# A decoder step on one core: decode key steps spread over two stages, their products over two engines, and norm operands moved to PSUM

## The chip, the cores and the metric

The kernel runs on one core of a Trainium2 chip. The core has a matrix engine (TensorE, PE in the profile, with its weight loads as PEld), a vector engine (VectorE, DVE), a scalar engine (ScalarE, ACT), a general engine (GpSimd, POOL) and a queue engine (SyncE, SP) that here issues all DMAs. Each engine takes its own instructions in the order in which the program gives them. The metric is the device time of one execution in microseconds.

## The reference

One inference step of a two-layer decoder, run for a prompt (1024 positions) and for 8 samples with one new position each, in float32, width 1024.

Layer 0 projects the input into queries, keys, values, gates and a pooling branch. Eight heads of 64 do stick-breaking attention:

```
z = q k^T / sqrt(64) + bias
log_keep = log_sigmoid(-z)            (only keys before the query)
w = exp(log_sigmoid(z) + sum of log_keep over the keys between this key and the query)
o = w v
```

The prompt attends to itself. Each sample attends to a cache of 4096 past keys and values, held in pages of 128 positions that a page table picks. The other branch is a multi-scale causal mean. Both are gated, projected by `w_out` and added to the input: `layer_norm(1.41 * x + o, g, b)`.

Layer 1 projects into three parts, gates one with another, runs a causal depthwise convolution with 31 taps, normalizes over the 1024 channels, applies SiLU, gates, projects by `w_out` and ends with the same kind of layer norm. The outputs are both groups' rows, the new keys and values, and the new pooling and convolution states.

## The kernel before, in words

Every float32 product of the projections is done as three products of split operands (high x high, high x low, low x high), so each weight piece is copied to a high part by ACT (line 205) and its rest is taken by POOL (line 210), and each activation is split likewise (lines 195 and 196). The prompt's rows stand in eight sets of 128 tokens.

The order on TensorE, ACT, DVE and POOL is the order in which the program emits instructions (`manual_schedule`); SP's queue is ordered by the framework's planner. The program runs in these stages:

1. A prologue, and then *attention* over 48 units (a head pair, a block of 128 queries, up to 512 keys). `z_a` makes the scores on TensorE and the sigmoids on ACT, `z_b` runs a scan and products on DVE (lines 365 to 371), `tpart` transposes the weights (line 845), `ppart` multiplies by the values (line 861). Between these, `fill.part` emits pieces of layer 0's input projection (lines 225 to 227).
2. The *out projection* of layer 0, `out_layer`: 32 groups of 24 matmuls (lines 1029 to 1031), each 128 tokens by 256 columns. After each group DVE adds the residual (line 1062) and takes statistics (1066). Two accumulators in PSUM, `acc()`, alternate; the first groups also use others. Once all four columns of a token set are done, its norm is put off for one or two groups and then emitted (`app`): a first op on DVE, (y - mean) x scale, `norm_a`; then either ACT and POOL, or on the fast path DVE again, for the factor of the deviation and the shift, `norm_b`. In layer 0 the scale stands in PSUM (`gps0`), so `norm_a` is two ops of 512 columns (line 1009); in layer 1 it stands in SBUF (line 1013).
3. Layer 1's input projection (`c_gen`) with the *convolution*: taps on DVE into a PSUM tile of two banks (`conv_acc`, tag "conv", line 1373) and on ACT and POOL; beside it `decode_v`, the samples' value products.
4. The *middle*: the convolution's norm. `mid_a` (lines 1555 and 1556) writes mean and deviation rows into one PSUM bank for each entry of `MID`, `mid_b` (line 1567) applies them on DVE, `mid_s` is SiLU on ACT, `mid_g` the gate on POOL or DVE (line 1588), `mid_c` the split (lines 195 and 196). PSUM banks shared for short use come from `trp()`, a ring of NZT banks in a pool that `swap_psum` replaces at each stage.
5. The *final projection* of layer 1, again `out_layer`, with the samples' path beside it, and the last norms.

Beside stages 1 and 2 runs `decode_k`, a generator of 155 steps that `tick(n)` advances. Two halves of 4 samples each have 64 units; a unit is two pages of keys. Step s loads unit s (line 405, four buffers `kt`), multiplies unit s - 2 by its query (line 417, on POOL or on DVE) and reduces unit s - 3 (line 409, DVE). After the 67 steps of a half come ten steps that finish it: transposes, sigmoids, a scan, a carry, and transposes back. The prologue gives 8 steps, each attention unit `TBASE + TSLOPE * (384 - keys) / 384`, each group of the out projection one, and the first 8 pieces of the next projection two each. What is then left runs alone.

Of the kernel before, what the change touches and what calls it, by code (L numbers as in the profile page):

```python
# [14 lines left out]
F32 = mybir.dt.float32  # L15
# [3 lines left out]
AF = mybir.ActivationFunctionType  # L19
ALU = mybir.AluOpType  # L20
AX = mybir.AxisListType
SP = mybir.EngineType.SP
PSUM = bass.MemoryType.PSUM

P = 128
D = 1024
S = 1024
# [18 lines left out]
KS = 30  # L46
PS_ = 15
NEG = -1e30
KMOD = 8
KPOOL = 7  # L50
ENG = mybir.EngineType
KLAG = 2
DTB = 2
# [12 lines left out]
WRB = 3  # L66
ETICK = 0.35
EDVE = (1, 2, 3, 0)
TBASE = 2.8
TSLOPE = 1.5  # L70
NHEADS = (0, 6, 6, 6, 6, 6, 6, 6)
SNY = 7
# [12 lines left out]
SNZ = 5  # L85
HALVES = (3, 6)
OLAG = 3
FAST = (5, 6, 7)
WCONVA = ((0, 5), (1, 5))
SY = 2  # L90
VRATE = 1.575
# [9 lines left out]
def kernel(  # L101
# [9 lines left out]
    pe, act, dve, gp, sp = nc.tensor, nc.scalar, nc.vector, nc.gpsimd, nc.sync  # L111
# [8 lines left out]
    w_out1 = w_out_c[0]  # L120
# [11 lines left out]
    pz = [pap.enter_context(tc.tile_pool(name="pza", bufs=1, space=PSUM))]  # L132
    NZT = [5]

    def psum(tag, bufs, shape=(P, 512), dt=F32):
        return (psq[0] if tag == "qv" else ps).tile(list(shape), dt, tag=tag, name=tag, bufs=bufs)
# [3 lines left out]
    def acc():  # L140
        deep[1] += 1
        if deep[0] and deep[1] % deep[0] == 0:
            return trp()
        return psum("acc", 2)

    def trp():
        return pz[0].tile([P, 512], F32, tag="zt", name="zt", bufs=NZT[0])

    def swap_psum(name, n):
        pzp.close()  # L150
        pz[0] = pzp.enter_context(tc.tile_pool(name=name, bufs=1, space=PSUM, reuse_waits="tile"))
        NZT[0] = n
# [63 lines left out]
    def dma_quarter(w, q, i):  # L216
        return dma_w(w[i * 256:(i + 1) * 256, q * 256:(q + 1) * 256], 2, 256)
# [171 lines left out]
    def decode_k():  # L389
        qrow = {0: query_rows(0)}  # L390
        yield
        for hf in range(2):
# [5 lines left out]
            for s in range(len(units) + KLAG + 1):  # L398
# [13 lines left out]
                if KLAG <= s < len(units) + KLAG:  # L412
                    bi, j = units[s - KLAG]
                    b = hf * 4 + bi
                    kt = kts[s - KLAG]
                    eng = gp if (j // 2) % KMOD < KPOOL else dve
                    eng.tensor_tensor(out=kt, in0=kt, in1=qrow[b], op=ALU.mult)  # L417
# [53 lines left out]
    def tick(n):  # L471
        while n > 0 and queue:
            try:
                next(queue[0])
                n -= 1
            except StopIteration:
                queue.pop(0)
# [328 lines left out]
    def z_a(u):  # L806
        pair, qb, c0, c1, first, last = units[u]
        n = c1 - c0
        nz = max(n, 256)
        km = KT[pair]  # L810
        sq, ql = SQ[pair, qb // 2]
        qs = slice(qb % 2 * P, qb % 2 * P + P)
        zs = [trp(), trp()]
        for hh in range(2):
            pe.matmul(zs[hh][:, 0:nz], sq[:, hh, qs], km[:, hh, c0:c0 + nz], start=True, stop=False)
        for hh in range(2):
            r = slice(hh * DH, hh * DH + DH)
            pe.matmul(zs[hh][:, 0:nz], ql[r, qs], km[r, hh, c0:c0 + nz], start=False, stop=not first)
        sk = []
        for hh in range(2):  # L820
            h = pair * 2 + hh
            if first:
                pe.matmul(zs[hh][:, n - P:n], identb, maskb, start=False, stop=True)
            kp = KP[u % 2 * 2 + hh]
            stick_a(zs[hh], kp, n, biash[:, h:h + 1], nbiash[:, h:h + 1])
            sk.append((zs[hh], kp))
        st["z", u] = sk
        if u in PREP:
            prep(*PREP[u])
# [62 lines left out]
    t = trp()  # L892
# [23 lines left out]
    for i, q in enumerate(qorder):  # L916
# [3 lines left out]
        o = acc()[:, 0:n]  # L920
# [26 lines left out]
    for u in range(len(units) + 2):  # L947
        if u < len(units):
# [6 lines left out]
            fcred += fbase  # L955
            tcred += TBASE + TSLOPE * (384 - n) / 384.0
            z_a(u)
# [47 lines left out]
    def norm_a(gb, y, mv, halves, gps):  # L1005
        if gps:
            for i in range(2):
                h = slice(i * 512, i * 512 + 512)
                dve.scalar_tensor_tensor(out=y[:, h], in0=y[:, h], scalar=mv[:, 0:1], in1=gps[i],
                                         op0=ALU.subtract, op1=ALU.mult)  # L1010
            return
        for h in halves:
            dve.scalar_tensor_tensor(out=y[:, h], in0=y[:, h], scalar=mv[:, 0:1], in1=gb[:, 0, h],
                                     op0=ALU.subtract, op1=ALU.mult)

    def norm_b(gb, y, rs, fast, h):
        if fast:
            dve.scalar_tensor_tensor(out=y[:, h], in0=y[:, h], scalar=rs, in1=gb[:, 1, h], op0=ALU.mult, op1=ALU.add)
        else:
            act.activation(out=y[:, h], in_=y[:, h], func=AF.Copy, scale=rs)  # L1020
            gp.tensor_tensor(out=y[:, h], in0=y[:, h], in1=gb[:, 1, h], op=ALU.add)  # L1021
# [10 lines left out]

    def out_layer(w, first, ahead, X, gb, pool, finish, between, before=None, half=None, tail=None, lag=OLAG, fast0=FAST, wide=0, gps=()):
        order = [(n4, tb) for t0 in (0, 4) for n4 in range(2) for tb in range(t0, t0 + 4)]
        for i in range(NTB + lag):
            if i < NTB:
                order.append((2, i))
            if i >= lag:
                order.append((3, i - lag))
        dmas = {0: (1, 3)} | {9 + i: (2, i) for i in range(4)} | {13 + i: (3, i) for i in range(4)}  # L1040
        convs = {i: (1, i) for i in range(4)} | {12 + i: (2, i) for i in range(4)} | {16 + i: (3, i) for i in range(4)}
        raws, sts = {}, {}
        tiles = {0: first, 1: [], 2: [], 3: []}

        def fetch(q, i):
            raws[q, i] = dma_quarter(w, q, i)

        for i in range(3):
            raws[1, i] = ahead[i]
        for s, (n4, tb) in enumerate(order):  # L1050
            f0 = n4 * 256
            if s in convs:
                q, i = convs[s]
                tiles[q].append(conv_w(raws[q, i], 2, 256, pool if q % 2 else None, dve if q == 1 and i % 2 and fast0 is FASTB else None))
            if s in dmas:
                fetch(*dmas[s])
            if before is not None:
                before(n4, tb)
            o = (trp() if s < wide and s % 3 else acc())[:, 0:256]
            out_group(tiles[n4], o, tb, half)  # L1060
            y = X[tb]
            dve.scalar_tensor_tensor(out=y[:, f0:f0 + 256], in0=y[:, f0:f0 + 256], scalar=ALPHA,
                                     in1=o, op0=ALU.mult, op1=ALU.add)
            if n4 == 0:
                sts[tb] = pool.tile([P, 4, 6], F32, tag="st", name="st", bufs=NTB)
            dve.bn_stats(sts[tb][:, n4, :], y[:, f0:f0 + 256])
            if n4 == 3:
                fast = tb in fast0
                halves = (slice(0, 512), slice(512, 1024)) if tb >= 6 else (slice(0, 1024),)
                mv, rs = norm_s(pool, sts[tb])  # L1070

                def app(y=y, mv=mv, rs=rs, tb=tb, fast=fast, halves=halves):
                    norm_a(gb[0], y, mv, halves, gps)
                    for h in halves:
                        norm_b(gb[0], y, rs, fast, h)
                        finish(tb, y, h)
                defer((DTC if fast0 is FASTB else DTD)[tb], app)
            between(n4, tb)
            point()
            if tail is not None:  # L1080
                tail(n4, tb)
# [4 lines left out]
    X = {}  # L1086
# [80 lines left out]
    rows = [(w_out0, 0, k) for k in range(NK)]  # L1167
# [347 lines left out]
    BC = {}  # L1515
# [34 lines left out]

    def mid_a(c):
        a, b = MID[c]
        t = trp()
        for i, tb in enumerate(range(a, b)):
            pe.transpose(out=t[:, i * P:(i + 1) * P], in_=rmf[:, tb:tb + 1].broadcast_to([P, P]), identity=ident)
            pe.transpose(out=t[:, 256 + i * P:256 + (i + 1) * P], in_=rvf[:, tb:tb + 1].broadcast_to([P, P]),
                         identity=ident)
        BC[c] = t
# [31 lines left out]
    X = {}  # L1590
# [5 lines left out]
            X[tb] = C[:, tb].rearrange("p k c -> p (k c)")  # L1596
            sp.dma_start(X[tb], x1_dram[tb * P:(tb + 1) * P, :])

    gb1 = [None]

    def before(n4, tb):
        if (n4, tb) in STEPS:
            STEPS[n4, tb]()
        if n4:
            return
        if tb == 3:
            gb1[0] = G[:, 0:2].rearrange("p t k c -> p t (k c)")
            sp.dma_start(gb1[0][:, 0, :], ln_c_g.to_broadcast([P, D]))
            sp.dma_start(gb1[0][:, 1, :], ln_c_b.to_broadcast([P, D]))
# [22 lines left out]
    mid_c(0)  # L1632
    mid_g(1)
    flush()
    swap_psum("pzd", 4)
    cxp.close()
    dx = ctx.enter_context(tc.tile_pool(name="dx", bufs=1, reuse_waits="tile"))
    fill.part(2)
# [9 lines left out]
    first1 = load_first(w_out1, range(2)) + late1  # L1648
    ahead1 = [dma_quarter(w_out1, 1, i) for i in range(3)]
# [3 lines left out]
    mid_g(2)  # L1653
    flush()
    deep[0] = DEEPD
    out_layer(w_out1, first1, ahead1, X, gb1, dx, fin1, lambda n4, tb: tick(1), before, lambda: tick(1))
    while queue:
        tick(1)
    flush()
# [24 lines left out]
```

## Time and profile before

| | |
|---|---|
| runs of the kernel before | 1143.98 us median of 3 (1140.2 to 1145.24) |
| the profiled execution | 1143.3 us, of which the span from first to last instruction is 1141.5 us |
| mean granted TensorE clock | 0.971 |
| attention | about 70 to 505 us |
| out projection with its norms | about 505 to 632 us |
| layer 1's projection with the convolution | about 632 to 960 us |
| middle | about 960 to 1012 us |
| final projection | about 1012 to 1127 us, last norms to 1141.5 us |

An engine's busy time is the time in which it has an instruction in work. Idle time of one engine matters only where another waits for it, so the waits and the timeline are read beside the busy times. The granted clock is a share of TensorE's full speed.

### The profile page before, as it was taken

What the parts mean: (1) busy time and instruction counts of PE and PEld (TensorE: products, weight loads), DVE (VectorE), ACT (ScalarE), POOL (GpSimd) and SP (SyncE); (2) the same over time, 40 slices, a digit from 0 to 9 for tenths busy, and PEclk for the clock granted to TensorE, in tenths of its full rate; (3) what the DMA queues carried; (4) which work ended last, traced back from release to release, by engine and by line L of the source; (5) the groups of instructions that cost most, each with busy time, mean ns of one, the idle gap of its engine ahead of it and who ended that gap; (6) DMA issues with size and microseconds to landing.
All of it is one profiled execution on the core that took longest, in us unless ns stands there. A gap on an engine that the chain in (4) does not pass through costs nothing.

```text
span 1141.5 us, 19830 instructions
## 1 busy us (share of the span) xinstructions
PE 1051.7 (92%) x6804; PEld 841.7 (74%) x6804; DVE 812.6 (71%) x961; ACT 491.9 (43%) x929; POOL 665.1 (58%) x502
## 2 busy tenths in 40 slices
PE   8998888889999998797998999999999999899994
PEld 7897777768877877697997666566666466677784
DVE  3458878688599898767348399999999960484246
ACT  4345465547565565571204224444544422462210
POOL 3277879691788889872418336765766612343235
PEclk9999999999999999898999999999999999899997
DMA  8577767783467976655203887787687678386922
GB/s 267 170 230 231 243 194 222 207 251 98 141 217 219 278 216 216 199 194 203 68 26 142 240 253 249 234 252 217 194 266 236 210 237 264 122 280 218 322 102 113
DMA packets 179206, 235.20 MB, mean 206 GB/s; under 512 B 15418, under 2 KB 95939, under 8 KB 179081
## 3 DMA queue, kind: packets, MB, share of 16 engines
q1 hardware_dynamic: 179105, 233.94, 65.1%
q8 instruction: 53, 0.87, 0.3%
q14 instruction: 48, 0.39, 0.1%
HBM read 212.60 MB, written 16.14 MB: 200 GB/s over the span
## 4 chain that ended last, share of the span: by engine, by line
PE 54%; POOL 13%; DVE 11%; issue 9%; DMA 7%; ACT 3%; SPq 3%; POOLq 0%; DVEq 0%; ACTq 0%
PE acc L225 11%; PE acc L227 10%; PE acc L226 10%; POOL kt L417 7%; PE qv L1151 5%; DMA kt<-in_cache_k_dram 3%; DVE zw L409 3%; PE acc L1029 3%; POOL wlo L210 2%; PE acc L1031 2%; PE acc L1030 2%; DVE kp L365 2%; DMA vt<-in_cache_v_dram 1%; DVE xl L196 1%; POOL xres L1021 1%
## 5 line engine op out<-in xcount | busy, mean ns | idle before, releaser
L225 PE MATMUL acc<-xh,whi 128*128 128x384 f32 (+2 forms) x960 | 361.5, 377 | 11.5 <-DVE hbt L705 5.7
L227 PE MATMUL acc<-xl,whi 128*128 128x384 f32 (+2 forms) x960 | 340.4, 355 | 0.2 <-DVE xl L196 0.2
L226 PE MATMUL acc<-xh,wlo 128*128 128x384 f32 (+2 forms) x960 | 339.7, 354 | 0.0
L417 POOL TENSOR_TENSOR kt<-kt,qbs 128x1024 f32<-128x1024 f32 x112 | 274.1, 2464 | 39.6 <-DMA kt<-in_cache_k_dram 30.0
L210 POOL TENSOR_TENSOR wlo<-wraw,whi 128x512 fp32r<-128x512 f32 x122 | 161.6, 1328 | 184.1 <-ACT whi L205 179.5
L1373 DVE SCALAR_TENSOR_TENSOR conv_acc<-hbuf,wdwT,conv_acc 128x1024 f32<-128x1024 f32 x196 | 252.8, 1290 | 6.8
L225 PEld LDWEIGHTS acc<-xh,whi 128*128 128x128 f32 x960 | 184.3, 192 | 78.1 <-issue 26.1
L409 DVE TENSOR_REDUCE zw<-kt 128x16 f32<-128x1024 f32 x128 | 153.6, 1212 | 63.5 <-POOL kt L417 63.3
L227 PEld LDWEIGHTS acc<-xl,whi 128*128 128x128 f32 x960 | 184.3, 192 | 18.0 <-DVE xl L196 0.7
L226 PEld LDWEIGHTS acc<-xh,wlo 128*128 128x128 f32 x960 | 185.0, 193 | 15.7 <-issue 0.3
L1363 POOL TENSOR_TENSOR conv<-conv,tap 128x512 f32<-128x512 f32 x84 | 105.9, 1293 | 17.6 <-ACT tap L1360 17.6
L1029 PE MATMUL acc<-whi,xh 128*128 128x256 f32 x352 | 102.4, 291 | 0.0
L1031 PE MATMUL acc<-whi,xl 128*128 128x256 f32 x352 | 99.5, 283 | 2.1 <-DVE xl L196 2.1
L1030 PE MATMUL acc<-wlo,xh 128*128 128x256 f32 x352 | 99.4, 282 | 0.0
L365 DVE TENSOR_TENSOR_SCAN kp<-kp,zt 128x512 f32<-128x512 f32 (+3 forms) x96 | 92.4, 963 | 1.2 <-ACT zt L361 1.2
L205 ACT ACTIVATE whi<-wraw 128x512 fp32r<-128x512 f32 x126 | 77.4, 624 | 32.1 <-DMA wraw<-in_w_out_ab_dram 14.1
L360 ACT ACTIVATE kp<-zt,nbiash 128x512 f32<-128x512 f32 (+3 forms) x96 | 55.8, 581 | 71.4 <-DVE sg L371 40.7
L1360 ACT ACTIVATE tap<-hbuf,wdwT 128x512 f32<-128x512 f32 x84 | 59.7, 721 | 48.0 <-POOL conv L1363 38.1
L1151 PE MATMUL qv<-vt,zw 128*32 128x512 f32 x512 | 76.1, 604 | 3.1 <-DMA vt<-in_cache_v_dram 3.1
L1029 PEld LDWEIGHTS acc<-whi,xh 128*128 128x128 f32 x352 | 66.8, 190 | 7.9 <-issue 7.4
L1031 PEld LDWEIGHTS acc<-whi,xl 128*128 128x128 f32 x352 | 67.0, 190 | 2.3 <-DVE xl L196 2.3
L845 PE MATMUL zt<-ident,sg 128*128 128x128 f32 x288 | 44.7, 286 | 24.2 <-DVE sg L371 12.9
(274 smaller groups left out, 1507.3 us busy)
## 6 DMA issues: line engine op xcount, KB each, us to landing
kt<-in_cache_k_dram SPq DMA_DIRECT2D x256, 256.0 KB
vt<-in_cache_v_dram SPq DMA_DIRECT2D x256, 256.0 KB
wraw<-in_w_in_c_dram SPq DMA_DIRECT2D x48, 256.0 KB
vt<-in_w_in_c_dram SPq DMA_DIRECT2D x48, 256.0 KB
wraw<-in_w_in_ab_dram SPq DMA_DIRECT2D x46, 256.0 KB
xt<-in_x_prompt_dram SPq DMA_DIRECT2D x8, 512.0 KB
wraw<-in_w_out_ab_dram SPq DMA_DIRECT2D x16, 256.0 KB
xres<-in_x_prompt_dram SPq DMA_DIRECT2D x8, 512.0 KB
```

The costliest lines, as they stand in the source:

```text
L210: (eng or gp).tensor_tensor(out=lo, in0=raw, in1=hi.bitcast(F32), op=ALU.subtract)
L225: pe.matmul(o, hi[:, k % 4, :], xh, start=(k == 0), stop=False)
L226: pe.matmul(o, lo[:, k % 4, :], xh, start=False, stop=False)
L227: pe.matmul(o, hi[:, k % 4, :], xl, start=False, stop=(k == NK - 1))
L365: dve.tensor_tensor_scan(out=kr, data0=kr, data1=z[:, 0:1].broadcast_to([P, n]), initial=1.0 if prev is None else prev, op0=ALU.mult, op1= ...
L409: dve.tensor_reduce(out=seg[:, j // 8, j % 8:j % 8 + 2, bi * 8:bi * 8 + 8], in_=kts.pop(s - KLAG - 1).rearrange("p a (h d) -> p a h d", d=DH),
L417: eng.tensor_tensor(out=kt, in0=kt, in1=qrow[b], op=ALU.mult)
L1029: pe.matmul(o, XH[:, k, cs], hi[:, k % 2, :], start=(k == 0), stop=False)
L1030: pe.matmul(o, XH[:, k, cs], lo[:, k % 2, :], start=False, stop=False)
L1031: pe.matmul(o, XL[:, k, cs], hi[:, k % 2, :], start=False, stop=(k == NK - 1))
L1151: pe.matmul(pv[32 * bi:32 * bi + 32, :], Z[:, j % 8 * 4 + j // 8, :], vts[bi], start=(j == 0), stop=(j == NPG - 1), tile_position=(0, 32 * ...
L1373: dve.scalar_tensor_tensor(out=part[1], in0=hb[:, j:j + S], scalar=w, in1=part[1], op0=ALU.mult, op1=ALU.add)
```

## The change

The decode keys advance by 2.35 steps a unit of 384 keys instead of 2.8. Three of four key products run on POOL and one on DVE, instead of seven and one of eight. The fast path of layer 1's norm serves token sets 5 and 7 instead of 5, 6 and 7.

A new `norm_fast` is used where the scale stands in PSUM and the token set is on the fast path: both first ops write to temporary PSUM banks, and both second ops read them there.

The rows of the first two entries of `MID` (token sets 0 and 1) go to the two banks of the convolution's accumulator. The final projection's ring of shared banks has three instead of four, and the bank set free, with the bank "o", holds layer 1's scale, copied by ACT before group (2, 4).

```
-KMOD = 8
-KPOOL = 7
+KMOD = 4
+KPOOL = 3
-TBASE = 2.8
+TBASE = 2.35
-FAST = (5, 6, 7)
+FAST = (5, 7)
...
+    def norm_fast(gb, y, mv, rs, h, i, gps):
+        t = trp()
+        dve.scalar_tensor_tensor(out=t, in0=y[:, h], scalar=mv[:, 0:1], in1=gps[i], op0=ALU.subtract, op1=ALU.mult)
+        return lambda: dve.scalar_tensor_tensor(out=y[:, h], in0=t, scalar=rs, in1=gb[:, 1, h], op0=ALU.mult, op1=ALU.add)
...
                 def app(y=y, mv=mv, rs=rs, tb=tb, fast=fast, halves=halves):
+                    if fast and gps:
+                        hs = (slice(0, 512), slice(512, 1024))
+                        bs = [norm_fast(gb[0], y, mv, rs, h, i, gps) for i, h in enumerate(hs)]
+                        for h, b in zip(hs, bs):
+                            b()
+                            finish(tb, y, h)
+                        return
                     norm_a(gb[0], y, mv, halves, gps)
...
     def mid_a(c):
         a, b = MID[c]
-        t = trp()
+        if c == 0:
+            BC["wide"] = pz[0].tile([P, S], F32, tag="conv", name="rows", bufs=1)
+        t = BC["wide"][:, c * 512:c * 512 + 512] if c < 2 else trp()
...
+        if (n4, tb) == (2, 4):
+            gps1.extend((psum("o", 1), pg.tile([P, 512], F32, name="scale1")))
+            for i in range(2):
+                act.activation(out=gps1[i], in_=gb1[0][:, 0, i * 512:i * 512 + 512], func=AF.Copy)
...
-    swap_psum("pzd", 4)
+    swap_psum("pzd", 3)
+    pg = ctx.enter_context(tc.tile_pool(name="pg", bufs=1, space=PSUM, reuse_waits="tile"))
...
-    out_layer(w_out1, first1, ahead1, X, gb1, dx, fin1, lambda n4, tb: tick(1), before, lambda: tick(1))
+    out_layer(w_out1, first1, ahead1, X, gb1, dx, fin1, lambda n4, tb: tick(1), before, lambda: tick(1), gps=gps1)
```

## Rows read from the trace of the kernel before

**Rows 1.** Busy time, share of the span and instructions of each engine, from the page.

```profile
PE 1051.7 (92%) x6804; PEld 841.7 (74%) x6804; DVE 812.6 (71%) x961; ACT 491.9 (43%) x929; POOL 665.1 (58%) x502
```

**Rows 2.** Stages: start:end and length, busy us (instructions) of each engine, clock, DMA share, GB/s.

```profile
core 0: us, PE busy (x) PEld busy (x) DVE busy (x) ACT busy (x) POOL busy (x), PEclk, DMA share, GB/s
70.00:505.00 435.00, 388.92 (x2651) 338.13 (x2651) 344.70 (x418) 244.37 (x509) 339.56 (x187) 0.96 0.69 212
505.00:590.00 85.00, 78.93 (x640) 78.25 (x639) 44.68 (x74) 20.43 (x38) 23.67 (x20) 0.96 0.32 111
590.00:632.00 42.00, 37.80 (x275) 34.22 (x273) 30.95 (x55) 17.74 (x27) 31.49 (x42) 1.00 0.39 133
...
1012.00:1127.20 115.20, 114.50 (x1000) 95.95 (x1000) 52.40 (x108) 28.75 (x49) 41.24 (x33) 0.99 0.60 205
```

**Rows 3.** Waits, 70 to 505 us: who waited for whom, us, times, longest.

```profile
PE zt L845 <- DVE sg L371: 12.9, 7, 3.2
PE zt L845 <- DVE sg L369: 10.8, 10, 2.4
...
DVE zw L409 <- POOL kt L417: 60.2, 32, 5.4
...
POOL kt L417 <- DMA kt<-in_cache_k_dram: 30.0, 22, 6.8
```

**Rows 4.** Busy us of line 417 (DVE, POOL), then of line 409 (DVE), by stretch.

```profile
70.00:505.00 435.00, 26.88 (x15) 261.61 (x107) 0.96 0.69 212
...
70.00:505.00 435.00, 146.10 (x122) 0.96 0.69 212
505.00:632.00 127.00, 3.60 (x3) 0.97 0.34 119
```

**Rows 5.** Lines' instructions: duration ns min/median/max, first and last start, shape.

```profile
L417 POOL TENSOR_TENSOR kt<-kt,qbs x112: 2337/2392/3387, 54.2 to 515.4; 128x1024 f32<-128x1024 f32 x112
L417 DVE TENSOR_TENSOR kt<-kt,qbs x16: 1209/1276/3224, 79.5 to 524.8; 128x1024 f32<-128x1024 f32 x16
...
L210 POOL TENSOR_TENSOR wlo<-wraw,whi x122: 1254/1291/2296, 28.6 to 1084.3; 128x512 fp32r<-128x512 f32 x122
...
L1009 DVE SCALAR_TENSOR_TENSOR xres<-xres,mv,qv x8: 737/740/744, 591.4 to 622.8; 128x512 f32<-128x512 f32 x8
...
L1013 DVE SCALAR_TENSOR_TENSOR conv<-conv,mv,gate x10: 740/1269/2382, 1099.9 to 1135.9; 128x1024 f32<-128x1024 f32 x6, 128x512 f32<-128x512 f32 x4
```

**Rows 6.** Two stretches of 10 us in attention, columns as in rows 2.

```profile
120.00:130.00 10.00, 5.42 (x29) 4.24 (x27) 8.71 (x10) 3.39 (x8) 8.59 (x5) 0.83 0.76 244
290.00:300.00 10.00, 10.00 (x73) 9.18 (x71) 3.21 (x8) 5.72 (x15) 5.42 (x6) 1.00 0.45 133
```

**Rows 7.** Timeline, DVE in the out projection: start, us, instruction, idle time before it.

```profile
570.10 0.42 DVE L1062 SCALAR_TENSOR_TENSOR xres<-xres,acc 128x256 f32<-128x256 f32 x1 [1.96 <-PE acc L1031]
...
572.94 0.42 DVE L1062 SCALAR_TENSOR_TENSOR xres<-xres,acc 128x256 f32<-128x256 f32 x1 [1.96 <-PE acc L1031]
```

**Rows 8.** Timeline: the decode's end (ACT, DVE), and the first norm's last set (DVE).

```profile
534.26 0.69 ACT L433 ACTIVATE kpd<-zt,nbiasd 128x512 f32<-128x512 f32 x1 [9.22 <-PE zt L429]
...
538.34 2.27 DVE L437 TENSOR_TENSOR_SCAN kpd<-kpd 128x1024 f32<-128x1024 f32 x1
...
623.42 3.18 DVE L1018 SCALAR_TENSOR_TENSOR xres<-xres,rs,lngb 128x512 f32<-128x512 f32 x2
```

**Rows 9.** Timeline around the norm rows and the final projection's start (TensorE, DVE).

```profile
987.79 0.45 PE L1555 MATMUL zt<-ident,rmu 128*128 128x128 f32 x1 [5.68 <-DVE conv L1567]
...
995.57 14.40 DVE L1567 TENSOR_TENSOR conv<-conv,zt 128x1024 f32<-128x1024 f32 x12
...
1012.30 0.38 PE L1031 MATMUL acc<-whi,xl 128*128 128x256 f32 x1 [2.09 <-DVE xl L196]
```

**Rows 10.** Timeline of the end (POOL, DVE).

```profile
1127.93 3.09 POOL L1021 TENSOR_TENSOR conv<-conv,gate 128x1024 f32<-128x1024 f32 x1 [0.43 <-ACT conv L1020]
...
1137.09 1.41 DVE L1018 SCALAR_TENSOR_TENSOR conv<-conv,rs,gate 128x512 f32<-128x512 f32 x2 [0.45 <-POOL rs L1002]
```

More of the change, by code (lines that the diff above doesn't have):

```diff
@@ L1597, in mid_c @@
             sp.dma_start(X[tb], x1_dram[tb * P:(tb + 1) * P, :])
-    gb1 = [None]
+    gb1, gps1 = [None], []
     def before(n4, tb):
```

## The prediction

> **What bounds the kernel now.** I read the page's engine totals first, then the busy times by stage, then the waits inside the stage that the change touches, then two timelines. The totals [rows 1] show TensorE busy for 92% of the span, so any time to be won is TensorE's idle time or time at its lower clock. By stage [rows 2] the idle time is uneven. In the attention stage (70 to 505 us) TensorE is busy 388.9 of 435 us, so it stands still for 46.1 us, and the mean granted clock is 0.96, which is 0.04 x 435 = 17.4 us of work lost to stretches at 1.2 GHz. In the final projection (1012 to 1127) it idles 0.7 us.
>
> Who holds TensorE up in the attention stage is in the waits [rows 3]: the two largest, 12.9 and 10.8 us, are transposes of the weights of attention that VectorE (DVE) has not finished. DVE in turn stood 60.2 us, 32 times, in front of the reduction of a decode key unit (line 409), waiting for GpSimd (POOL) to finish the product of that unit (line 417). DVE takes its instructions in order, so the scans and products of attention stand behind that reduction. POOL spent 261.6 us of the stage in 107 such products [rows 4] and was busy for 339.6 of 435 us. A check from inside the trace: from 290 to 300 us, where no more than a few decode steps run (POOL busy 5.4 of 10 us), TensorE has no idle time, and from 120 to 130, with POOL at 8.6 and DVE at 8.7, it is busy 5.4 of 10 at clock 0.83 [rows 6]. So the decode steps, through POOL and the order of DVE's queue, cost TensorE time here; the stage is not limited by its matmuls.
>
> The out projection that follows (505 to 590) is the opposite: DVE 44.7 and POOL 23.7 of 85 us [rows 2].
>
> **The change, part by part.**
>
> *Steps moved.* The loop hands out 2.8 steps a unit, 48 units of 384 keys in the mean, so 134; with the 8 of the prologue that is 142. The three reductions after 505 us [rows 4] confirm it (the 143rd to 145th step). At 2.35 it hands out 112. So 22 steps leave the attention stage: of 122 reductions there 100 stay, and of 122 products 75 on POOL and 25 on DVE, against 107 and 15. POOL loses 32 x 2.44 = 78 us (339.6 to 261, 60% of the old stage). DVE loses 22 x 1.20 = 26.3 us of reductions and gains 10 x 1.79 = 17.9 us of products [rows 4], so 8.4 us less. The 60.2 us in front of the reduction I halve: the pressure on POOL falls by a quarter, but its own waits for key loads, 30.0 us [rows 3], have other causes. DVE then has 8 + 30 = 38 us more air in the stage. The two largest of TensorE's waits for DVE alone make 23.7 of its 46.1 us of idle time [rows 3]. I take 20 us as gone, and 4 of the 17.4 us of clock, since the clock falls after idle stretches [rows 6]: -24 us. The ends: 63 us if all idle and clock loss went; a loss of 7 if the DVE products cost what the first rival says.
>
> *Where they land.* From the first group of the out projection on, one step runs behind each of its 32 groups, so there are 25 reductions and 24 products (18 POOL, 6 DVE) in groups 0 to 24 instead of 3 and 2. Groups come every 2.84 us, and DVE idles 1.96 us of each [rows 7]. A reduction of 1.20 and a quarter of a 1.79 us product take 1.65, so DVE still fits, with 0.3 us to spare. POOL's share is 0.75 x 2.44 = 1.83 us a group; in the ten or so groups that also split a weight piece on POOL (1.29 us each [rows 5]) that makes 3.1, over the 2.84, so POOL falls behind by some 0.3 us a group there: 3 us. With two accumulators TensorE waits only once DVE is a group late. With some waits before it I take +5 (ends 0 and +30; the upper is the second rival's mechanism at six tenths). The first three groups pay nothing new: a reduction stood behind each of them before. On the queue of SP, 44 key loads move to this stage and each waits for a reduction; the residual rows and weight quarters stand behind them. The DMA engines are 0.32 busy there [rows 2] and a quarter is requested three groups ahead, 8.5 us, so nothing, at worst +3.
>
> *The end of the decode.* After the last reduction comes a tail: four sigmoids of 0.69 us on ACT, a scan of 2.27 us on DVE, transposes, a multiply [rows 8]. It moves from groups 5 to 13, where all of it was hidden, to groups 27 to 31 and the first two pieces of the next projection, where norms run and POOL is 31.5 of 42 us busy [rows 2]. The scan stands in front of a norm that POOL waits for. +3 us (0 to +8, the upper being scan and sigmoids and as much again for the rest).
>
> *The first norm.* The fast path now also serves its last token set. Its two second ops took 3.18 us beside POOL's sums [rows 8]; read from PSUM I price them like other ops with one operand there, 0.74 each [rows 5], so 1.7 us, of which I count 1, because the transposes of set 6 wait as well: -1 (0 to -1.7).
>
> *Norm rows in the convolution's banks.* Before, TensorE stands for 5.68 us before the rows of sets 2 to 4 [rows 9], because a bank is held until DVE has read set 1's rows. With sets 0 and 1 in the convolution's banks this wait can go, yet what is late next is unchanged: the third group of the final projection stops for the split of set 2 until 1012.30 [rows 9], and that split stands on DVE behind twelve norm ops that start at 995.57, which no part of the change moves. So 0 (+1 if three banks instead of four bind; the gain end is the fourth rival).
>
> *Second norm's scale in PSUM.* Two copies on an idle ACT: hidden. On DVE a whole set's first op costs 2 x 0.74 = 1.48 instead of 1.27, or of up to 2.38 beside POOL [rows 5]. Only the last stretch, after TensorE's end, is on the path. There set 6's second ops leave DVE: 1.41 and 0.45 of waiting, as the last set's ops have them [rows 10], 1.9 together; one stretched first op shrinks by about 1.1. Against it set 6's sum joins POOL, where a sum took up to 3.09 [rows 10] and the last set's root stands behind it; DVE is late enough to cover most of that. -3 (0 to -5).
>
> Sum: -24 + 5 + 3 - 1 - 3 = -20, on the profiled run's 1143.3 us (span 1141.5). The median of the three runs is 0.7 above it, so 1124 us.
>
> **A rule that speaks against it.** DVE's product of two operands in SBUF took 1.21 to 3.22 us and POOL's 2.34 to 3.39 [rows 5], so they stretch each other. The Trainium skill, SBUF — State Buffer, section "Who interferes with whom", states it harder: a DVE instruction with two SBUF inputs and a GpSimd instruction that reads SBUF cannot run together, and the one that comes second is blocked for the whole of the first. By that rule every product moved to DVE could wait out a whole POOL product; the mean in the trace, 1.79, is far from that, and the sum by the rule is the first rival's.
>
> **The rivals.**
> 1. *The products block each other.* Each of 25 DVE products in the attention stage waits a whole POOL product: 1.21 + 2.39 = 3.60 instead of 1.79, 45 us more on DVE, over the 38 gained. Attention gains nothing: +5 + 3 - 1 - 3 = +4, 1148 us. For it: the 3.22 us maximum. Against: the median of 1.28, with POOL busier than it will be [rows 5]. Chance 0.08.
> 2. *Slower: the out projection's evacuations stand behind reductions that wait for POOL.* If POOL is not ahead, each reduction waits a product, 2.39 us, on top of DVE's 2.84 - 1.96 = 0.88 and 1.65: 4.9 instead of 2.84 us a group, so 2.1 x 24 = 50 us in place of the 5. It decides as soon as the wait passes 0.3 us a group; in the attention stage it was 60.2 / 122 = 0.49. With half of that price, +25: 1144 us; with two thirds, +33, 1152 us; in full 1169. I take 1155. Against: POOL was busier in attention, and two accumulators cover a group. Chance 0.10.
> 3. *All of TensorE's idle time in attention goes*: -46 instead of -24: 1102 us. For it the stretch at 290 us. Chance 0.10.
> 4. *The rows' wait does count*: 5.68 and about 3 us of clock behind it: 1115 us. Against: the later stop at 1012.30. Chance 0.05.
> 5. *The waits in attention are latency, not load*: a third of the gain, -8: 1140 us. Chance 0.08.
>
> **How the numbers follow.** The forecast has 0.59, with a range of its own from 1112 to 1136. What can be told from no change is 0.5%, 5.7 us. Faster than 1138.3 us: 0.57 of the forecast, rivals 3 and 4, and 0.03 of the fifth: 0.75. Slower than 1149.7: 0.09 of the second, 0.01 of the first: 0.10. The rest, 0.15, is the same. The range from 1104 to 1148 leaves out most of the second rival, half of the third and half of the first, about 0.2.
>
> **What would show it.** Right: 25 reductions after the first matmul of the out projection; DVE's wait for POOL in front of line 409 at 20 to 40 us; TensorE idle below 30 us between 70 us and the end of attention; groups at 2.84 to 3.1 us; the third group of the final projection still stopped by set 2's split; DVE's last op about 8 us after TensorE's last matmul, against 11 (1138.5 after 1127.2). Wrong: DVE products with a mean above 2.5 us (rival 1), or TensorE waiting on evacuations in the out projection for over 20 us (rival 2).

## The result, and the profile after

The changed kernel takes 1117.3 us (median of four runs, 1115.3 to 1118.7) where the kernel before takes 1144.6 beside it on the same chip: a ratio of 0.9768, 95% interval 0.9739 to 0.9797, so faster by 27 us. The forecast was 1124 us with a range of 1104 to 1148. The profiled execution took 1117.6 us, with a span of 1115.8.

The engine totals of the changed kernel, from the page, to set beside [rows 1]:

```profile
PE 1041.7 (93%) x6804; PEld 835.9 (75%) x6804; DVE 833.3 (75%) x982; ACT 493.8 (44%) x933; POOL 632.2 (57%) x488
```

TensorE is 10 us less busy with as many matmuls: that is clock, not work. Next come the stretches of the changed kernel, cut at its own milestones: attention (to the first matmul of the out projection), on to the first evacuation, groups 0 to 23, the rest of the groups, and on to the first tap of the convolution. Columns as in [rows 2].

```profile
70.00:467.90 397.90, 376.69 (x2662) 330.11 (x2662) 330.27 (x408) 245.17 (x512) 268.39 (x156) 1.00 0.67 204
467.90:482.20 14.30, 12.38 (x105) 12.18 (x103) 14.17 (x12) 7.28 (x14) 11.10 (x7) 1.00 0.30 99
482.20:549.80 67.60, 61.56 (x488) 60.85 (x489) 57.56 (x78) 6.70 (x11) 50.76 (x25) 0.92 0.81 275
549.80:587.90 38.10, 31.05 (x229) 30.53 (x227) 28.11 (x49) 14.74 (x21) 22.07 (x21) 0.87 0.18 67
587.90:626.40 38.50, 32.39 (x156) 23.73 (x154) 12.40 (x20) 12.33 (x22) 18.81 (x33) 0.91 0.54 173
```

The kernel before, cut at the same milestone of attention:

```profile
70.00:507.20 437.20, 391.12 (x2670) 340.33 (x2670) 346.90 (x421) 246.03 (x512) 340.90 (x188) 0.96 0.69 211
```

Attention is 39.3 us shorter. Of these, 24.9 are idle time of TensorE (437.2 - 391.1 = 46.1 before, 397.9 - 376.7 = 21.2 after), and 14.4 are busy time, as the clock is 1.00 instead of 0.96. Then 17.8 us are given back: from the first out-projection matmul to the first tap it takes 158.5 us instead of 140.7. The rest barely moves until the end, where the stretch behind the last matmul is 10.8 us instead of 14.3.

The waits of the changed kernel in attention (who waited for whom, us, times, longest), against [rows 3]:

```profile
DVE zw L409 <- POOL kt L417: 29.9, 19, 3.8
...
POOL kt L417 <- DMA kt<-in_cache_k_dram: 18.1, 8, 4.1
...
PE zt L845 <- DVE sg L371: 8.7, 9, 1.4
```

DVE's wait for POOL is halved, and TensorE's longest wait for DVE's weights of attention fell from 3.2 to 1.4 us.

Where the time was given back is in TensorE's timeline from 550 us on. These are its stops in the norms (start, us, instruction, and in brackets the idle time before it and who ended it):

```profile
560.27 1.97 PE L1138 MATMUL zt<-ident,xres 128*128 128x128 f32 x8 [3.44 <-POOL xres L1026]
...
581.76 1.09 PE L1138 MATMUL zt<-ident,xres 128*128 128x128 f32 x8 [3.61 <-POOL xres L1026]
...
591.66 0.19 PE L451 MATMUL zt<-ident,crow 1*128 1x1 f32 x1 [2.16 <-DVE xl L196]
...
598.48 1.97 PE L463 MATMUL zt<-ident,zw 128*128 128x128 f32 x8 [3.60 <-DVE xl L196]
```

Line 1138 transposes a normed token set; lines 451 and 463 are transposes of the decode's end. Before, the same norms held TensorE four times, 3.2 us in all, never over 1.0. From evacuation 23 (the end of the 24th group) to the first tap, the kernel before and then the changed one:

```profile
587.14:647.93 60.79, 56.59 (x377) 47.57 (x375) 33.37 (x61) 21.98 (x35) 37.07 (x48) 1.00 0.47 152
```

```profile
549.76:626.41 76.65, 63.50 (x382) 54.31 (x381) 40.55 (x68) 27.07 (x44) 40.92 (x53) 0.89 0.36 121
```

Of the 15.9 us that this part grew by, 9.0 are idle time of TensorE (4.2 to 13.2) and 6.9 busy time, as the clock is 0.89 instead of 1.00. The second stop can be followed back on DVE, ACT and POOL:

```profile
571.81 3.73 DVE L437 TENSOR_TENSOR_SCAN kpd<-kpd 128x1024 f32<-128x1024 f32 x1
575.47 1.26 DVE L196 TENSOR_TENSOR xl<-zt,xh 128x512 fp32r<-128x512 f32 x2
576.64 0.73 DVE L1009 SCALAR_TENSOR_TENSOR xres<-xres,mv,o 128x512 f32<-128x512 f32 x1
...
578.13 1.15 ACT L1025 ACTIVATE xres<-xres,rs 128x1024 f32<-128x1024 f32 x1 [5.96 <-DVE xres L1009]
...
571.00 2.40 POOL L1026 TENSOR_TENSOR xres<-xres,lngb 128x1024 f32<-128x1024 f32 x1 [1.55 <-ACT xres L1025]
573.36 2.20 POOL L1001 TENSOR_SCALAR rs<-mv 128x1 f32<-128x1 f32 x1
575.64 0.57 POOL L1002 TENSOR_TENSOR rs<-rs,mhalf 128x1 f32<-128x1 f32 x1
579.35 2.35 POOL L1026 TENSOR_TENSOR xres<-xres,lngb 128x1024 f32<-128x1024 f32 x1 [3.14 <-ACT xres L1025]
```

The decode's scan (line 437) stands on DVE ahead of the split (196) and of the norm's first op (1009). So ACT's step of the norm starts only at 578.13, POOL's sum at 579.35, and TensorE's transposes when that is done.

### The profile page after: what moved, and what is told of

It is laid out like the page before. It is cut to its first block, busy times and chain, and to the rows that moved or that the text cites. A ratio compares the mean times of both kernels' runs of the same rounds, so it can differ in the third digit from the quotient of the medians.

```text
span 1115.8 us, 19853 instructions
## 1 busy us (share of the span) xinstructions
PE 1041.7 (93%) x6804; PEld 835.9 (75%) x6804; DVE 833.3 (75%) x982; ACT 493.8 (44%) x933; POOL 632.2 (57%) x488
## 4 chain that ended last, share of the span: by engine, by line
PE 44%; DVE 11%; POOL 7%; issue 5%; DMA 4%; ACT 3%; SPq 2%; DVEq 0%; POOLq 0%; ACTq 0%
PE acc L225 9%; PE acc L227 8%; PE acc L226 8%; PE qv L1163 6%; POOL kt L417 3%; DMA kt<-in_cache_k_dram 2%; DVE zw L409 2%; DVE conv L1581 2%; PE acc L1034 2%; DVE xl L196 2%; PE acc L1035 1%; PE acc L1036 1%; PE qv L1199 1%; PE zt L1034 1%; POOL wlo L210 1%
## 5 line engine op out<-in xcount | busy, mean ns | idle before, releaser
L417 POOL TENSOR_TENSOR kt<-kt,qbs 128x1024 f32<-128x1024 f32 x96 | 240.5, 2518 | 64.5 <-DMA kt<-in_cache_k_dram 35.0
L227 PEld LDWEIGHTS acc<-xl,whi 128*128 128x128 f32 x960 | 181.9, 190 | 17.8 <-DVE xl L196 0.4
L226 PEld LDWEIGHTS acc<-xh,wlo 128*128 128x128 f32 x960 | 182.4, 190 | 16.0 <-POOL wlo L210 0.2
L1035 PEld LDWEIGHTS acc<-wlo,xh 128*128 128x128 f32 x352 | 68.0, 193 | 2.0 <-POOL wlo L210 1.9
```

The costliest lines, as they stand in the source:

```text
L226: pe.matmul(o, lo[:, k % 4, :], xh, start=False, stop=False)
L227: pe.matmul(o, hi[:, k % 4, :], xl, start=False, stop=(k == NK - 1))
L1035: pe.matmul(o, XH[:, k, cs], lo[:, k % 2, :], start=False, stop=False)
```

## Experiments

A ratio is always against the kernel before, run beside it. Milestones are read from each run's trace; "attention" is from 70 us to the first out-projection matmul, and "the norm stretch" from there to the first tap.

**Which part of the change gives the time.** Four kernels: the share of products alone, the rate alone, both, and everything else alone.

```diff
 share:  -KMOD = 8 / KPOOL = 7     +KMOD = 4 / KPOOL = 3     (on the kernel before)
 rate:   -TBASE = 2.8              +TBASE = 2.35             (on the kernel before)
 keys:   both of these                                       (on the kernel before)
 psum:   both of these taken back                            (on the changed kernel)
```

> The kernel before with three of four key products on GpSimd instead of seven of eight; the rate stays 2.8 steps a unit, and nothing else changes. If the wait for GpSimd's load is what costs attention its idle time (theory), GpSimd loses 15 products of 2.5 us in attention, DVE's wait in front of the key reduction falls from 60 to about 45 us, and the run is 5 to 10 us shorter than before. If the DVE products pay for a whole GpSimd product (rival), it is not shorter, or slower by up to 10 us.

> The kernel before with the rate of 2.35 steps a unit alone. Theory: most of the 39 us that attention lost in the changed kernel come from the 22 steps that leave it, so attention is 25 to 35 us shorter, some 15 us of that go again between the first out-projection matmul and the first convolution tap, and the run is 12 to 20 us shorter than before. Rival: the share of products is what counts, then under 8 us.

> The kernel before with both the rate of 2.35 and three of four products on GpSimd, none of the PSUM parts. Theory: attention as in the changed kernel (first out-projection matmul near 468 us), the run 22 to 24 us shorter than before (1120 to 1122), the rest of the change's 27 us being the PSUM parts. Rival: the PSUM parts bring the out-projection stage or the rows more than 5 us, then this one stands above 1123.

> The changed kernel with the old rate (2.8) and the old share (seven of eight): the PSUM parts alone. Theory: 3 us between the last matmul and the end, 0 to 1 from the rows, 1 from the first norm: 3 to 5 us shorter than before. Rival (rows' wait counts): 8 us or more shorter, with the third group of the final projection no longer stopped.

| kernel | ratio (95%) | median us | attention us | norm stretch us | behind the last matmul us |
|---|---|---|---|---|---|
| before | 1 | 1141.5 | 437.2 | 140.7 | 14.3 |
| share | 1.0091 (1.0056 to 1.0126) | 1151.9 | 442.0 | 141.8 | 14.3 |
| rate | 0.9820 (0.9768 to 0.9871) | 1122.8 | 399.7 | 157.8 | 14.3 |
| keys | 0.9820 (0.9772 to 0.9868) | 1122.4 | 398.1 | 160.6 | 14.3 |
| psum | 1.0018 (0.9992 to 1.0043) | 1143.7 | 436.1 | 144.2 | 10.9 |
| changed | 0.9768 (0.9739 to 0.9797) | 1117.3 | 397.9 | 158.5 | 10.8 |

The rate does most of it, and the share of products nothing: alone it makes the kernel slower by 0.9%, and its theory fell. Beside the new rate it changes nothing either (0.9820 with and without). What the changed kernel wins over that, 0.9768 against 0.9820, is not clear of the intervals; the traces show 3.5 us of it behind the last matmul. The waits of the share kernel, 70 to 512 us:

```profile
POOL kt L417 <- DMA kt<-in_cache_k_dram: 43.7, 24, 5.2
...
DVE zw L409 <- POOL kt L417: 35.3, 18, 5.5
...
PE zt L845 <- DVE sg L371: 12.8, 8, 4.2
...
PE zt L845 <- DVE sg L369: 11.9, 13, 3.4
```

and its attention:

```profile
70.00:512.00 442.00, 394.54 (x2672) 342.33 (x2671) 372.04 (x434) 246.62 (x512) 313.50 (x173) 0.96 0.68 209
```

POOL is 27 us less busy, and waits 14 us longer for its keys. DVE waits 25 us less for POOL and is busy 25 us more. What it waited before, it works now: the sum of both is 407 us here as it was before (346.9 + 60.2 and 372.0 + 35.3). The rival's reason for a slower kernel, DVE products that each pay a whole POOL product, isn't it either: they take 1.79 us in the mean, as before (53.82 us for 30). TensorE's waits for DVE are as long as in [rows 3].

The PSUM parts alone give no difference. Behind the last matmul they win 3.4 us, as forecast; between the last evacuation of the out projection and the first tap they lose as much, 34.1 us instead of 30.7. TensorE's stop there, and the sum that finishes the token set which it waits to transpose, in the timeline of the psum kernel:

```profile
623.29 1.30 PE L1138 MATMUL zt<-ident,xres 128*128 128x128 f32 x8 [4.25 <-DVE xres L1019]
...
617.60 2.38 POOL L1026 TENSOR_TENSOR xres<-xres,lngb 128x1024 f32<-128x1024 f32 x1 [0.41 <-ACT xres L1025]
```

`norm_fast` keeps the intermediate of set 7 in two banks of the ring that the transposes of the sets before it also take. Set 5 was finished by POOL at 619.98, yet its transposes, the sixth of eight groups, come only behind line 1019, which frees the banks.

**What the decode's end costs, and where it stands.** One kernel leaves it out, one puts it eight steps later, and two change the rate.

```diff
 no end:  +            if hf == 1:
          +                for _ in range(10):
          +                    yield
          +                continue
 later:   -            for _ in range(SY):           (ahead of the second half's transposes)
          +            for _ in range(SY + 8 * hf):
 2.5:     -TBASE = 2.35     +TBASE = 2.5
 2.2:     -TBASE = 2.35     +TBASE = 2.2
```

> The changed kernel without the end of the second half of the decode (its sigmoids, scan, multiplies and transposes are left out, ten empty steps stand in their place, so the sample outputs of four sequences are not those of the reference). Theory: the 17.8 us that the stretch from the first out-projection matmul to the first convolution tap grew by are this end, standing beside the first norms, so 12 to 16 us of them go and the run is at 1101 to 1105 us. Rival: they are the key steps in the groups of the out projection; then 3 us at most go (1114 us).

> The changed kernel with eight empty steps more ahead of the end of the second half, so that its sigmoids, scan and transposes come after the last norms, with the first pieces of the next projection. Theory (the place beside the norms is what costs): TensorE's stops of 3.4 and 3.6 us before the transposes of the norms go, 8 to 12 us are won and the run is at 1105 to 1109 us. Rival (the end costs wherever it stands, as TensorE waits in its own order for the transposes of the end): within 4 us of the changed kernel.

> The changed kernel at 2.5 steps a unit: eight key steps go back into attention, and the end of the decode falls on groups 16 to 27, mostly ahead of the norms. Theory: attention loses 8 x 39.3 / 22 = 14 us, and 10 to 14 of the 18 us after it come back: 1117 to 1122 us. Rival (the last steps taken from attention gave little, as the first ones took most of the idle time): attention loses only 5 us, and the run is at 1108 us.

> The changed kernel at 2.2 steps a unit: seven key steps more leave attention, and the reductions run to group 31, so that they stand beside the norms and the end of the decode comes after the norms. Theory: attention gains 7 to 12 us more; beside the norms stand six reductions of 1.2 us in place of a scan of 3.7 us and four sigmoids, so the stretch after it is no longer than now or up to 5 us shorter: 1103 to 1112 us. Rival (attention has nothing left to give, as its remaining 21 us of idle time have other causes): 1114 to 1120 us.

| kernel | ratio (95%) | median us | attention us | norm stretch us |
|---|---|---|---|---|
| no end | 0.9720 (0.9700 to 0.9741) | 1111.7 | 396.9 | 151.0 |
| later | 0.9746 (0.9716 to 0.9775) | 1114.9 | 399.5 | 153.6 |
| 2.5 | 0.9870 (0.9848 to 0.9893) | 1127.7 | 420.2 | 145.8 |
| 2.2 | 0.9994 (0.9974 to 1.0014) | 1140.8 | 404.6 | 173.5 |

Without the end the norm stretch is 7.5 us shorter, half of what I expected. (The median of the whole run falls by 5.6 us; in the trace 4 us are lost again between the first tap and the last matmul, and why was not followed.) So the end is less than half of the 17.8 us. In that kernel the first of the stops stays and one for the first norm's banks shows, by its own line numbers (1023 is line 1019 of the changed kernel):

```profile
559.22 1.09 PE L1142 MATMUL zt<-ident,xres 128*128 128x128 f32 x8 [3.43 <-POOL xres L1030]
...
588.83 1.11 PE L1142 MATMUL zt<-ident,xres 128*128 128x128 f32 x4 [3.16 <-DVE xres L1023]
```

So the first stop does not come from the end. DVE's rows ahead of it, in the changed kernel, show the last key steps in front of the first norm:

```profile
550.67 0.26 DVE L999 BATCH_NORM_AGGREGATE mv<-st 128x2 f32<-128x24 f32 x1
550.98 1.22 DVE L409 TENSOR_REDUCE zw<-kt 128x16 f32<-128x1024 f32 x1
552.12 1.21 DVE L417 TENSOR_TENSOR kt<-kt,qbs 128x1024 f32<-128x1024 f32 x1
...
554.04 1.20 DVE L409 TENSOR_REDUCE zw<-kt 128x16 f32<-128x1024 f32 x1
555.16 0.74 DVE L1009 SCALAR_TENSOR_TENSOR xres<-xres,mv,o 128x512 f32<-128x512 f32 x1
```

From the set's statistics (line 999) to its first norm op it takes 4.5 us here, and took 2.7 before (588.05 to 590.78). At 2.5 steps, where the last reduction comes at 552 us and the first norm op at 575, no stop of TensorE behind POOL's sum is over 1.0 us. The later end wins about 5 us in the stretch (the stop of 3.61 us is gone, that of 3.44 stays), but the interval of its ratio overlaps that of the changed kernel: not shown to be faster.

At 2.5 steps the end falls mostly ahead of the norms and the stretch is 5.1 us longer than before, 3.5 of it as in the psum kernel. But attention loses 22 us, against 14 expected. At 2.2 attention did not go on falling: it is longer than at 2.35, the norm stretch is the longest of all, and the whole gain is gone (0.9994). Both forecasts for the rates failed.

**What is left in attention, and the first norm.**

```diff
 first norm:     -                    if fast and gps:
                 +                    if fast and gps and fast0 is not FASTB:
 later + first:  this and the later end
 2.3:            -TBASE = 2.35     +TBASE = 2.3       (on later + first)
 no keys:        -TBASE = 2.35 / TSLOPE = 1.5     +TBASE = 0.0 / TSLOPE = 0.0
```

> The changed kernel with the first norm's last token set as before the change (its first ops write their result back over the residual rows in SBUF, not into two banks of the transposes). Theory: in the run of the PSUM parts alone this path held the transposes of the set before it for 4.25 us and the stretch from the last evacuation to the first convolution tap grew from 30.7 to 34.1 us; in the changed kernel the end of the decode stands in the same place, so 0 to 3 us are won: 1114 to 1117 us. Rival (the forecast's own step: the path saves 1 us): 1118 us, and no wait for line 1019 goes.

> The end of the decode eight steps later and the first norm's last set as before the change. Theory: the two costs add up, so from the kernel with the later end another 3 us go, as TensorE's 3.1 us wait for line 1019 goes: 1111 to 1113 us, last evacuation to first tap 36 to 37 us in place of 39.9. Rival (another wait takes its place): 1114 to 1116 us.

> As the run before it, at 2.3 steps a unit: two or three more key steps leave attention. Theory (2.35 is near the least: from 2.5 to 2.35 attention fell by 22 us, and at 2.2 it was 7 us longer again, by stretches at the lower clock): within 4 us of the run before, 1109 to 1116 us. Rival (each step that leaves is worth the 2.8 us that those between 2.5 and 2.35 were): 1104 to 1107 us.

> The changed kernel with no key step handed out in attention's units; they come in the groups of the out projection and in one stretch ahead of the convolution, so the whole run will be far longer and only attention is read. Theory (the key steps are what holds TensorE up there): TensorE idles under 8 us from 70 us to the end of attention, at clock 0.99 to 1.00, and the first out-projection matmul comes at 445 to 455 us instead of 467.9. Rival (the 21 us left in the changed kernel have other causes): idle stays at 18 us or more, first matmul at 463 to 468 us.

| kernel | ratio (95%) | median us | attention us | norm stretch us |
|---|---|---|---|---|
| first norm | 0.9786 (0.9763 to 0.9809) | 1118.8 | 397.0 | 158.9 |
| later + first | 0.9757 (0.9734 to 0.9780) | 1114.5 | 397.6 | 155.0 |
| 2.3 | 0.9921 (0.9900 to 0.9943) | 1134.7 | 413.1 | 160.3 |
| no keys | one run | 1320.7 | 367.0 | not read |

The first norm's path costs 3.4 us where it is the only thing in its place, and nothing that can be measured once the decode's end stands there too. In later + first TensorE's wait for line 1019 is gone, and another takes its place, the first transposes of the decode's end (waits of TensorE in its norm stretch, and DVE's timeline):

```profile
PE zt L1138 <- POOL xres L1026: 5.1, 4, 2.8
PE zt L429 <- DVE xl L196: 5.0, 1, 5.0
```

```profile
587.87 3.12 DVE L1023 SCALAR_TENSOR_TENSOR xres<-xres,rs,lngb 128x512 f32<-128x512 f32 x2
590.92 1.27 DVE L196 TENSOR_TENSOR xl<-zt,xh 128x512 fp32r<-128x512 f32 x2
```

In the kernel with the later end alone this second wait was 0.6 us. The split that TensorE waits for stands on DVE behind the old path's second ops, which take 3.12 us again.

Without key steps TensorE idles 1.6 us in all of attention:

```profile
70.00:437.00 367.00, 365.36 (x2637) 326.65 (x2636) 172.58 (x281) 240.74 (x503) 80.20 (x78) 1.00 0.27 74
```

So nearly all of the 21 us of idle time still in the changed kernel are the key steps' too. The first out-projection matmul comes at 437.0 us, earlier than the 445 to 455 expected.

At 2.3 steps attention is 15.5 us longer than at 2.35 with the rest of the kernel alike, though two fewer reductions stand in it. One long stop and what follows it, in that kernel's timeline and stretches:

```profile
411.72 1.25 PE L713 MATMUL zt<-hbt,wpool 128*128 128x264 f32 x2 [3.96 <-DVE hbt L705]
```

```profile
410.00:415.00 5.00, 3.09 (x11) 1.77 (x13) 4.86 (x9) 0.69 (x3) 4.13 (x2) 0.52 0.74 248
415.00:420.00 5.00, 5.00 (x19) 4.67 (x19) 4.86 (x7) 2.11 (x5) 3.02 (x5) 0.50 0.35 115
```

Behind the stop of 3.96 us the granted clock is 0.5, the lower level of 1.2 GHz, until about 420 us. In the changed kernel no stop of TensorE in attention is longer than 1.6 us, and the clock is 1.00 in the mean.

## Why the prediction was right or wrong

| step | forecast us | measured us | from |
|---|---|---|---|
| attention: idle time | -20 | -24.9 | 46.1 to 21.2 |
| attention: clock | -4 | -14.4 | busy 391.1 to 376.7 |
| key steps in groups 0 to 23 | +5 | +1.9 | first matmul to evacuation 23: 80.0 to 81.9 |
| end of the decode, first norm | +3 - 1 | +15.9 | from there to the first tap: 60.8 to 76.7 |
| convolution, norm rows | 0 | -0.7 | to the last matmul: 479.3 to 478.6 |
| second norm, behind the last matmul | -3 | -3.5 | 14.3 to 10.8 |
| sum | -20 | -25.7 | spans, 1141.5 to 1115.8 |

The forecast was right in sign and in its main mechanism, fewer key steps in attention. That it came near in size is luck: attention gave 15 us more than forecast, and the end of the decode with the first norm took 14 us more.

**Attention.** The mechanism held: DVE's wait in front of the reduction went from 60.2 to 29.9 us (20 to 40 was named as the sign), 25 reductions came behind the first out-projection matmul, and TensorE's idle time ended below 30. But the reason given was two things in one, fewer steps and a lighter POOL. The share kernel shows that the second is worth nothing here: the work that leaves POOL appears on DVE, and TensorE waits for DVE.

The mis-sized term is the clock: 4 of the 17.4 us that it cost were counted, and 14.4 came back. The rates show how (the first row is the kernel before, with its own share of products, the fourth is on later + first, the last has no key step in attention's units):

| steps a unit | reductions ahead of the out projection | attention us | stops of TensorE of 2 us and more | clock in attention |
|---|---|---|---|---|
| 2.8 | 125 | 437.2 | 7 | 0.96 |
| 2.5 | 111 | 420.2 | 4 | 0.98 |
| 2.35, seven kernels | 103 | 396.9 to 399.7 | none | 0.99 to 1.00 |
| 2.3 | 101 | 413.1 | 3 | 0.98 |
| 2.2 | 96 | 404.6 | 3 | 0.98 |
| none | 4 | 367.0 | none | 1.00 |

A line through 2.8, 2.5, 2.3 and 2.2 falls by 1.07 us a reduction and gives 413 at the 103 of 2.35. So by that line the 22 steps that left are worth 24 us, the forecast's figure, and 15 us more come with this one rate. The line is rough, one trace a rate, and it holds for this range alone: at 4 reductions it would give 307. Of the five rates the lucky one, 2.35, is the one without long stops, and its clock is the highest. Nothing in the forecast counts on that. Why the steps fall so well there was not settled; no run moved them at a constant count.

**Where the steps land.** The groups of the out projection took them more cheaply than forecast, 1.9 us instead of 5: the groups come every 2.94 us in the mean ((549.76 - 482.22) / 23 evacuations; before, 2.90 taken the same way), DVE had room for them (57.56 of 67.6 us busy), and the slower rival (evacuations behind reductions that wait for POOL, 1155 us) did not come. At 2.2 steps it begins to show: TensorE waits 2.40 us for the evacuation ahead of 550.59, and the same part takes 88.8 us.

**The end of the decode** is the step that failed: +3 was forecast from the scan and the sigmoids as DVE and ACT time. What counts is the queue behind each: the scan delays a norm that passes DVE, ACT, POOL and TensorE in turn, and the transposes of the end stop TensorE itself in its own order (2.16 and 3.60 us, behind DVE's split of line 196, which reads banks of their ring). Leaving the end out returns 7.5 us. The remaining 8.4 of the 15.9 are the last key steps beside the first norms (the stop of 3.44 us, which stays without the end), the lower clock behind the stops (0.87 and 0.91), and the first norm. By kind, 9.0 of the 15.9 are idle time and 6.9 clock; by cause I can't split them, as they overlap: taking away one lets another show.

**The first norm** was forecast at -1. Its two second ops did fall to 1.4 us, from the 3.18 of [rows 8], but the banks that hold its intermediate are those of the transposes: +3.4 by itself, hidden in the changed kernel. The forecast counted the op and not the bank.

**The norm rows** are worth nothing, as forecast. The rows of sets 2 and 3 no longer wait, but the stop only moves: it is 5.24 us, ahead of the rows of the sets behind them. The third group of the final projection still stops for the split of set 2. The timeline of the changed kernel, against [rows 9]:

```profile
960.07 0.27 PE L1569 MATMUL zt<-ident,rmu 128*128 128x128 f32 x1
...
965.91 0.45 PE L1569 MATMUL zt<-ident,rmu 128*128 128x128 f32 x1 [5.24 <-DVE conv L1581]
...
990.44 0.38 PE L1036 MATMUL acc<-whi,xl 128*128 128x256 f32 x1 [2.53 <-DVE xl L196]
```

**The last norms** went as forecast; DVE's last op ends 8 us after the last matmul (1112.86 after 1104.96), against [rows 10]. One price in that sum was misread, without weight: a stretched first op falls from 2.38 to 1.48, by 0.9 and not by 1.1. DVE's last op:

```profile
1111.45 1.41 DVE L1019 SCALAR_TENSOR_TENSOR conv<-zt,rs,gate 128x512 f32<-128x512 f32 x2 [1.32 <-POOL rs L1002]
```

**The first rival**, products that block each other, fell in size: DVE's 25 products in attention took 1.44 us in the mean and not 3.60. The last section shows that its lock is there all the same.

## What to carry to other kernels

When background work is spread over a stage by a rate, try neighbouring rates before believing one: 2.3 and 2.35 differ by 1.6% here, more than half of what the whole change gave. Price work that moves by the queues it stands in and by the buffers that it holds, not by its duration: a scan of 2.3 us stood behind a stop of 3.6 us of TensorE three engines further on, where 0.9 is left without the decode's end. And moving work from a busy engine to the one that waits for it won nothing here, as that one feeds the critical engine.

## What the runs showed of the hardware

A DVE op and a POOL op that meet hold each other up for the rest of the one that came first, less 0.1 us in these rows. In the changed kernel a POOL product and a DVE product met so, with POOL first:

```profile
160.89 2.21 DVE L417 TENSOR_TENSOR kt<-kt,qbs 128x1024 f32<-128x1024 f32 x1
...
159.63 2.38 POOL L417 TENSOR_TENSOR kt<-kt,qbs 128x1024 f32<-128x1024 f32 x1
```

The POOL product had 159.63 + 2.38 - 160.89 = 1.12 us to go, and the DVE product took 2.21, which is that and 1.09, near the 1.21 that it takes alone. Here DVE was first:

```profile
89.67 1.21 DVE L417 TENSOR_TENSOR kt<-kt,qbs 128x1024 f32<-128x1024 f32 x1
89.73 3.41 POOL L417 TENSOR_TENSOR kt<-kt,qbs 128x1024 f32<-128x1024 f32 x1
```

The DVE product had 1.15 us to go, and the POOL product took 3.41, which is that and 2.26, near the 2.39 that it takes alone. In the rows around 571.81 above it goes both ways: the scan starts 1.59 us before POOL's sum ends and takes 3.73 instead of 2.27, and POOL's tiny add at 573.36 (0.22 elsewhere) takes 2.20 and ends at 575.56, with the scan's end at 575.54. The Trainium skill, SBUF — State Buffer, section "Who interferes with whom", calls the port pair that the two engines share an exclusive lock, has a DVE instruction with two SBUF inputs contend with a GpSimd instruction that reads SBUF, and lets the order of issue decide who is blocked; these rows agree. Blocked for the whole of the first, as the prediction has it, is the most that this can come to.

What made the first rival too dear is that it let every DVE product wait, and for a whole POOL product. Of the 25 in attention 18 took no more than 1.23 us and 7 took 1.72 to 2.45, so DVE lost 36.1 - 25 x 1.21 = 5.9 us. They do meet often: ten POOL products that met one of them took 2.78 to 3.42 us, and there DVE had come first and POOL paid.
